# Four 32-row fp32 products for the samples' new SSD states, and B turned by a DMA transpose, in a hybrid attention and SSD layer

## The chip, the cores and the metric

The kernel runs on one core of a Trainium2 chip. The time is the device time of one execution in microseconds (us), taken as the median of several executions. One more execution was recorded by the hardware profiler; durations of single instructions come from that one. TensorE is the matrix engine (PE in the profile; PEld is its weight loads), VectorE is DVE, ScalarE is ACT, GpSimd is POOL, and SP issues most of the DMAs. Each engine works through its own instruction list in order, and semaphores hold an instruction back until what it needs is there. TensorE writes its results to PSUM, from where DVE or ACT must fetch them before the bank can be used again.

## What is computed

One streaming step of one layer serves a prompt of 1024 tokens and 8 samples of 16 tokens each: 1152 tokens together. An input projection feeds a chunk-band attention and a state-space branch (SSD, 32 heads in 4 groups), which are gated, merged and projected. The part that the change touches is the step of the SSD scan, in which each sample is one chunk of 16 tokens:

```python
cb = jnp.einsum('blgn,bsgn->blsg', ck, bk)
...
y_st = jnp.einsum('blgn,bgepn->blgep', ck, h) * jnp.exp(a_cs)[..., None]
to_end = jnp.exp(a_cs[:, -1:] - a_cs)
h_new = h * jnp.exp(a_cs[:, -1])[..., None, None] + jnp.einsum('blgn,blgep->bgepn', bk, xdt * to_end[..., None])
```

`bk` is the matrix B of a group (tokens by 128 states n), `x` the inputs of the heads, `h` the state. For each sample and each pair of heads the second term of `h_new` is a product of B (16 tokens by 128) with the weighted inputs (16 tokens by 128, two heads of 64), summed over 16 tokens. All outputs are fp32.

## The kernel before

**Dense products.** Nearly all of TensorE's time goes into projections whose operands are split into a high and a low fp16 part. One block of 128 output rows takes 3 token groups of 384 columns, 8 slices of the contraction and three matmuls each (L872 high by high, L873 high by low, L875 low by high; L925 to L927 are the same for attention, and L781 to L783 for the last projections, with 288 columns). The results go to three PSUM banks named `d`; three more, `g`, and a double bank, `s`, serve everything else.

**SSD.** After the 8 attention units come 4 groups of 4 pairs of heads. For each group a generator, `group_lat`, prepares what the group's pairs share: B with the tokens on the partitions (`tok`) and the masked product of C and B (`cbm`). B comes out of the convolution with its 128 states on the partitions, so it has to be turned: nine 128 by 128 fp32 transposes on TensorE (L1848), in three rounds that alternate with the products of B and C (L1854); ACT fetches the turned B (L1849) and DVE masks the product (L1856). For each pair, `prelude` makes the decay matrices, and `main` turns the pair's inputs x by a DMA transpose: ACT parts the fp32 words into two planes of 16 bits (L1940), SP starts the transpose (L1942), DVE joins the planes again (L1944). Then come the state products of the prompt (L1990), the outputs within the chunks (L2018, on halves of the array's columns), those from the samples' states (L2025) and from the prompt's (L2038), the store of y (L2055), and at last the samples' new states.

**The samples' new states before.** Two samples of 16 tokens share 32 rows of the 128. B and the weighted inputs `xw` are split into fp32r parts, each 64-row half once as high and once as low: `hi`, `lo` of B once per group (L1962 to L1965), `t` of the inputs per pair (L1971, L1972). GpSimd copies `t` four times with all rows but one sample's masked to zero, two samples in a tile (L1979, `masked(q)`, q = 0 to 3). TensorE then multiplies 128 rows by 256 columns eight times: for each q once with `hi` and once with `lo` (L2063). Only two masked tiles have room, so `masked(2)` and `masked(3)` wait for the products of q = 0 and 1, and there is a pause between the two halves. DVE adds the products to the states (L2072), and they are stored (L2081).

**What sets the order.** Generators record the program with estimated pauses. A list scheduler, class `Order`, then lays out each engine's list once more: from estimated costs of every instruction, it takes the unit that can start first, with a margin after a wait for another engine or a DMA where other work is at hand. So an edit to the SSD part moves instructions on all engines from that place to the end; the order before it, and the set of dense products, stay. Nothing is rearranged when the kernel runs.

**After SSD** come the remaining gate projections, the attention projection with 288 columns, beside which `mod_gate` makes the last modulation vectors (L1004 on quarters of the array's columns, fetched by ACT in L2283, then L1010), and the final projections. ACT's list there also has the splits of the SSD outputs (L2141), which DVE normalises first (L2231) with factors that arrive by a DMA from `yb`.

Of the kernel before, what the change touches and what calls it, by code (L numbers as in the profile page):

```python
# [7 lines left out]
F32 = mybir.dt.float32  # L8
# [3 lines left out]
U16 = mybir.dt.uint16  # L12
I32 = mybir.dt.int32
AF = mybir.ActivationFunctionType
ALU = mybir.AluOpType

P = 128
D = 1024
KT = D // P
NP = 1024  # L20
NB = 8
NS = 16
# [16 lines left out]
TURN = 9000  # L39
# [7 lines left out]

NQL = NQ + 32

C_ID, C_U, C_UB, C_ONE, C_BLK, C_BM, C_SEL, C_S4, C_BM4 = 0, 128, 256, 384, 512, 640, 648, 680, 712  # L50
NCONST = 716

PARAMS = [("norm_g", KT), ("b_ada", 24), ("conv_w", NCV * 4), ("conv_b", NCV), ("qk_g", 2), ("dskip", NPAIR),
          ("ssd_g", NPAIR), ("dt_bias", 32), ("a_log", 32)]
# [366 lines left out]
def trunk_kernel(ctx: ExitStack, tc: tile.TileContext, h, again):  # L421
    nc = tc.nc
# [3 lines left out]
    pss = ctx.enter_context(tc.tile_pool(name="pss", bufs=1, space=bass.MemoryType.PSUM))  # L426
# [4 lines left out]
    rarena = Arena(sb.tile([P, 1280], F32R, name="rarena"), 1280)  # L431
# [4 lines left out]
    def nm(s):  # L436
        uid[0] += 1
        return f"{s}{uid[0]}"

    def pg(cols=512):  # L440
        return psg.tile([P, 512], F32, tag="g", name=nm("g"))[:, :cols]
# [9 lines left out]
    cst = fix(NCONST)  # L451
# [17 lines left out]
    ident = cst[:, C_ID:C_ID + P]  # L469
# [5 lines left out]
    sel = cst[:, C_SEL:C_SEL + 32]  # L475
    sel4 = cst[:, C_S4:C_S4 + 9]
    bmask4 = cst[:, C_BM4:C_BM4 + 4]

    HN = NT // 2
    NSLOT = 12  # L480
# [28 lines left out]
    n = (HCOLS - E0 - 3 * 1184 - 1024) // 1184  # L509
# [5 lines left out]
    more = arena.set_layout(E0 + 1184 + NP + 2048, [("T", 2, NT), ("S", 4, 640)])  # L515
    for tag in more:
        L_ATT[tag] = L_ATT[tag] + more[tag]
    L_ST = rarena.set_layout(0, [("b", 4, P), ("s", 2, P), ("x", 2, 2 * P)])

    def alloc(lay, tag, cols):  # L520
        if lay is L_H or lay is L_W or lay is L_W3 or lay is L_Q or lay is L_V or lay is L_WQ or lay is L_WD:
            return Buf(arena, arena.alloc(lay, tag, cols // 2), cols, True)
        if lay is L_ST:
            return Buf(rarena, rarena.alloc(lay, tag, cols), cols)
        if (lay is L_SSD or lay is L_HEAD or lay is L_TAIL) and tag == "T" or lay is L_HEAD and tag == "Y":
            try:
                return Buf(arena, arena.alloc(L_MORE, "T", cols), cols)
            except NoSlot:
                pass
        return Buf(arena, arena.alloc(lay, tag, cols), cols)  # L530
# [4 lines left out]
    def walloc(lay, tag, cols):  # L535

        while True:
            try:
                return alloc(lay, tag, cols)
            except NoSlot as x:  # L540
                blocked[0] = str(x)
                yield None
# [25 lines left out]
    dma = nc.sync.dma_start  # L568
# [369 lines left out]
    for k in range(KT):  # L938
        b = alloc(L_START, "T", NT)
# [41 lines left out]
    sq = [alloc(L_START, "T", NT) for _ in range(2)]  # L981
# [3 lines left out]
    for k in range(1, KT):  # L985
# [5 lines left out]
        x = xs_in[k].ap  # L991
# [112 lines left out]
    x = xs_in[0]  # L1104
    rp = [psd.tile([P, G3], F32, tag="d", name=nm("d")) for _ in range(3)]
    for g, tok in enumerate(groups):

        for j in range(3):
            late(nc.tensor.matmul(rp[g][:, j * P:(j + 1) * P], v[1][:, 3 * g + j:3 * g + j + 1].to_broadcast([P, P]), ident,
                                  start=True, stop=True))  # L1110
# [12 lines left out]
    sp = pss.tile([P, 2, 512], F32, tag="s", name=nm("s"))  # L1123
# [15 lines left out]
    for k in range(KT):  # L1139
        if k == 0:  # L1140
# [25 lines left out]
            for i in range(3):  # L1166
# [3 lines left out]
                b = wraw[1 + i] = alloc(L_RAW, "raw", 1024)  # L1170
# [58 lines left out]
    def until(t):  # L1229
        while clock[0] < t:  # L1230
            yield -1.0

    def pause(t):
        yield from until(clock[0] + t)
# [78 lines left out]
    def planes(x, at, n):  # L1313
        return x.ap[:, at:at + n * P].bitcast(U16).rearrange("p (t k) -> p t k", t=2)

    def words(x, at, n):
        return x.ap[:, at:at + n * P].bitcast(U16).rearrange("p (k t) -> p t k", t=2)
# [510 lines left out]
    grp = {}  # L1828

    def group_dense(g, lay):  # L1830
        res = grp[g] = {"b": [], "c": [], "sq": None, "st": None}
        yield from conv_gen(16 + g, lay, res["b"])
        yield from conv_gen(20 + g, lay, res["c"])

    def group_lat(g):
        yield from ready(lambda: g in grp and grp[g]["c"] and att_left[0] == 0)
        res = grp[g]
        bt, ct = res["b"][0][0], res["c"][0][0]
        tok = yield from walloc(L_SSD, "T", NT)
        cbm = yield from walloc(L_SSD, "T", NT)  # L1840
        yield from until(res["c"][0][1])
        for j in range(3):
            n = min(4, 9 - 4 * j)
            c = slice(4 * j * P, (4 * j + n) * P)
            pt = pg()
            for s in range(n):
                t0 = (4 * j + s) * P
                nc.tensor.transpose(pt[:, s * P:(s + 1) * P], bt.ap[:, t0:t0 + P], ident)  # L1848
            nc.scalar.activation(tok.ap[:, c], pt[:, :n * P], AF.Copy)  # L1849
            yield 107 * n  # L1850
            pc = pg()
            for s in range(n):
                t0 = (4 * j + s) * P
                nc.tensor.matmul(pc[:, s * P:(s + 1) * P], bt.ap[:, t0:t0 + P], ct.ap[:, t0:t0 + P], start=True, stop=True)  # L1854
            m = (upper if j < 2 else upperb).unsqueeze(1).to_broadcast([P, n, P])
            nc.vector.tensor_tensor(cbm.ap[:, c].rearrange("p (s l) -> p s l", l=P),  # L1856
                                    pc[:, :n * P].rearrange("p (s l) -> p s l", l=P), m, ALU.mult)
            yield 213 * n
        bt.free()
        res["ct"], res["tok"], res["cbm"] = ct, tok, cbm  # L1860
# [3 lines left out]
    def ssd(p):  # L1864
        st = {}
        g = p // PPG
# [60 lines left out]
        def main():  # L1927
            yield from ready(lambda: ssd_all[p] and "z" in st and "cbm" in grp[g] and "t" in dts and st["x"])
            x, tx = st["x"][0]
            z = st["z"]  # L1930
            res = grp[g]
            tokb, ct = res["tok"], res["ct"]
            xd = yield from walloc(lay, "T", NT)
            xw = yield from walloc(lay, "T", NT)
# [17 lines left out]
            me, eb, h0, tm = st["me"]  # L1952
            ssd_all[p + 1] = True

            if res["st"] is None:
                bs = res["st"] = []
                for j in range(2):
                    rw, ro = slice(64 * j, 64 * j + 64), slice(64 - 64 * j, 128 - 64 * j)
                    b_ = tokb.ap[rw, NP:]
                    hi = yield from walloc(L_ST, "b", P)  # L1960
                    lo = yield from walloc(L_ST, "b", P)
                    nc.scalar.activation(hi.r[rw], b_, AF.Copy)  # L1962
                    nc.scalar.activation(hi.r[ro], b_, AF.Copy)
                    nc.vector.tensor_tensor(lo.r[rw], b_, hi.ap[rw], ALU.subtract)
                    nc.vector.tensor_tensor(lo.r[ro], b_, hi.ap[rw], ALU.subtract)  # L1965
                    bs.append((hi, lo))
            xs = []
            for j in range(2):
                rw, ro = slice(64 * j, 64 * j + 64), slice(64 - 64 * j, 128 - 64 * j)
                t = yield from walloc(L_ST, "s", P)  # L1970
                nc.scalar.activation(t.r[rw], xw.ap[rw, NP:], AF.Copy)  # L1971
                nc.vector.tensor_tensor(t.r[ro], xw.ap[rw, NP:], t.ap[rw], ALU.subtract)  # L1972
                xs.append(t)

            def masked(q):

                t = alloc(L_ST, "x", 2 * P)
                i = 2 * (q % 2)
                nc.gpsimd.tensor_tensor(t.r.rearrange("p (b n) -> p b n", n=P), xs[q // 2].ap.unsqueeze(1).to_broadcast([P, 2, P]),  # L1979
                                        bmask4[:, i:i + 2].unsqueeze(2).to_broadcast([P, 2, P]), ALU.mult)  # L1980
                return t

            xm = [masked(0), masked(1)]

            yield from pause(1500)
            for j in range(2):
                ps = pg()
                for s in range(4):
                    c = 4 * j + s
                    nc.tensor.matmul(ps[:, s * P:(s + 1) * P], tokb.ap[:, c * P:(c + 1) * P], xw.ap[:, c * P:(c + 1) * P],  # L1990
                                     start=True, stop=True)
# [64 lines left out]
            nc.scalar.activation(z.ap, x.ap, AF.Square)  # L2056
            stored(x)
            yield from pause(2000)
            pss_ = [pg(), pg()]
            for q in range(4):  # L2060
                j, i = q // 2, q % 2
                for w, b_ in enumerate(res["st"][j]):
                    nc.tensor.matmul(pss_[j][:, 2 * i * P:2 * (i + 1) * P], b_.r, xm[q].r, start=w == 0, stop=w == 1)  # L2063
                xm[q].free()
                if q < 2:
                    xm.append(masked(q + 2))
                yield 215
                if q == 1:
                    yield from pause(4500)
                if i:  # L2070
                    c = slice(4 * j * P, (4 * j + 4) * P)
                    nc.vector.tensor_tensor(h0.ap[:, c], h0.ap[:, c], pss_[j], ALU.add)  # L2072
            for t in xs + [xw]:
                t.free()
            if res["sq"] is None:
                res["sq"] = z
            else:
# [4 lines left out]
            stored(h0)  # L2082
            if p % PPG == PPG - 1:
                s = res["sq"]
                for t in (tokb, res["cbm"], res["ct"], *res["st"][0], *res["st"][1]):
                    t.free()
                yield from pause(4500)
                r0 = drp.tile([1, NT], F32, name=nm("ya"))
                r1 = res["r"] = drp.tile([1, NT], F32, name=nm("yb"))
                yield from token_sums(ones[:, :32], 1, s, r0)  # L2090
                yield from rsqrt_dram(r0, r1, 1, 512, nb)
                if p == NPAIR - 1:
                    dts["x"].free()
# [2133 lines left out]
```

## Time and profile before

| | |
|---|---|
| median of 3 runs | 1749.53 us (1746.5 to 1753.16) |
| the profiled execution: time | 1750.06 us |
| the profiled execution: span of its instructions | 1748.3 us |
| mean granted TensorE clock | 0.995 |
| DMA queue 1 (SP), share of 16 engines | 52.4% |
| SSD part with the remaining gates, us from the start | about 640 to 1360 |

The span begins with the first instruction and ends with the last. In the profile, a row of the groups gives the line of the kernel, the engine, the operation, the tiles and shapes, the count, and then the busy time in us and the mean duration of one in ns. A matmul's duration includes the time until its last result is out, and matmuls overlap; what one costs in a stream is the distance from its start to the start of the next. An fp32 matmul appears as two records (8 records are 4 products); an fp32r or fp16 matmul and a transpose as one. A timeline row gives the start, the length, the engine, line and shapes, the number of instructions merged, and in brackets idle time of the engine with what ended it.

### The profile page before, as it was taken

The page shows a single profiled execution, that of the slowest core. Times are in us where ns is not written, and L with a number is a line of the kernel's source. Part 1 is how long each engine was busy: PE and PEld are TensorE (multiplying, and loading weights), DVE is VectorE, ACT ScalarE, POOL GpSimd, SP SyncE. Part 2 cuts the span into 40 slices and gives each one's busy share as a digit, 9 for nine tenths or more (in the row PEclk, how much of TensorE's full clock was granted, in tenths as well). Part 3 has the DMA queues.
Part 4 walks back from the last instruction along what each step waited for, and adds up shares of the span by engine and source line. Part 5 has one row for each costly group of instructions (what it writes and reads, how often), then busy time and mean ns, then how long its engine had stood idle before and what let it go on. Part 6 is the DMA issues. An engine that isn't in the chain of part 4 may idle for free.

```text
span 1748.3 us, 35611 instructions
## 1 busy us (share of the span) xinstructions
PE 1718.8 (98%) x14013; PEld 1113.4 (64%) x14013; DVE 1312.6 (75%) x2477; ACT 995.8 (57%) x1987; POOL 351.4 (20%) x624
## 2 busy tenths in 40 slices
PE   7999999999999999999999999999999999999998
PEld 3556556556556566667666766676666677666676
DVE  6458667877776967787878777777778787897694
ACT  8766555566465665655755556555666633455340
POOL 0233233224134011232312122212112200000000
PEclk9999999999999999999999999999999999999999
DMA  9248888988878584643554355434555655421141
GB/s 383 76 126 204 191 218 204 200 221 196 203 226 173 148 214 133 171 131 118 170 160 116 118 133 175 140 117 108 155 165 194 244 192 222 146 89 54 58 157 72
DMA packets 267433, 284.92 MB, mean 163 GB/s; under 512 B 199724, under 2 KB 200376, under 8 KB 267256
## 3 DMA queue, kind: packets, MB, share of 16 engines
q1 hardware_dynamic: 258296, 253.90, 52.4%
q0 software_dynamic: 8960, 28.65, 4.4%
q8 instruction: 112, 1.84, 0.4%
q14 instruction: 65, 0.53, 0.1%
HBM read 192.70 MB, written 43.66 MB: 135 GB/s over the span
## 4 chain that ended last, share of the span: by engine, by line
PE 87%; ACT 4%; DVE 4%; DMA 2%; issue 1%; POOL 1%; SPq 0%; DVEq 0%; ACTq 0%; POOLq 0%
PE d L872 16%; PE d L873 16%; PE d L875 16%; PE d L925 5%; PE d L927 5%; PE d L926 5%; PE g L1531 2%; PE s L2018 2%; PE g L1990 2%; PE g L2038 1%; PE s L783 1%; PE s L781 1%; PE s L782 1%; PE s L1578 1%; PE g L1578 1%
## 5 line engine op out<-in xcount | busy, mean ns | idle before, releaser
L872 PE MATMUL d<-arena 128*128 128x384 f16 x1872 | 611.8, 327 | 1.4 <-ACT arena L1706 1.4
L873 PE MATMUL d<-arena 128*128 128x384 f16 x1872 | 610.7, 326 | 0.0
L875 PE MATMUL d<-arena 128*128 128x384 f16 x1872 | 610.7, 326 | 0.0
L875 PEld LDWEIGHTS <-arena 128*128 128x128 f16 x1896 | 185.7, 98 | 122.9 <-issue 0.5
L872 PEld LDWEIGHTS <-arena 128*128 128x128 f16 x1896 | 185.7, 98 | 121.5 <-issue 8.6
L873 PEld LDWEIGHTS <-arena 128*128 128x128 f16 x1896 | 185.7, 98 | 113.5 <-issue 2.0
L628 ACT ACTIVATE arena<-arena 128x1024 bf16<-128x1024 f32 (+4 forms) x185 | 184.6, 998 | 106.1 <-DMA arena<-in_wall_dram 65.4
L925 PE MATMUL d<-arena 128*128 128x384 f16 (+1 forms) x568 | 186.8, 329 | 0.0
L637 DVE SCALAR_TENSOR_TENSOR arena<-arena 128x1024 f16<-128x1024 f32 (+2 forms) x133 | 160.0, 1209 | 35.1 <-ACT arena L636 33.3
L927 PE MATMUL d<-arena 128*128 128x384 f16 (+1 forms) x568 | 186.1, 328 | 0.0
L926 PE MATMUL d<-arena 128*128 128x384 f16 (+1 forms) x568 | 186.1, 328 | 0.0
L636 ACT ACTIVATE arena<-arena 128x1024 f16<-128x1024 f32 (+2 forms) x133 | 135.5, 1021 | 85.3 <-PE d L873 15.5
L1471 ACT ACTIVATE arena<-arena 128x640 f32<-128x640 f32 (+4 forms) x144 | 100.8, 701 | 62.9 <-DVE arena L1474 62.4
L1729 DVE SCALAR_TENSOR_TENSOR arena<-arena 128x1176 f32<-128x1176 f32 x72 | 107.3, 1490 | 2.3 <-issue 0.9
L1917 ACT ACTIVATE arena<-arena 128x128 f32<-128x128 f32 x288 | 89.9, 390 | 25.9 <-DMA arena<-acs_d 25.7
L925 PEld LDWEIGHTS <-arena 128*128 128x128 f16 x576 | 56.3, 98 | 50.8 <-issue 17.5
L1507 DVE SCALAR_TENSOR_TENSOR arena<-arena 128x640 f16<-128x640 f32 (+4 forms) x128 | 87.0, 713 | 0.0
L1366 ACT ACTIVATE arena<-d 128x256 f32<-128x256 f32 x71 | 26.8, 377 | 96.1 <-PE d L927 96.0
L927 PEld LDWEIGHTS <-arena 128*128 128x128 f16 x576 | 56.4, 98 | 38.4 <-issue 0.2
L1399 POOL TENSOR_SCALAR arena<-arena 128x16 f32<-128x16 f32 (+1 forms) x24 | 9.4, 392 | 353.5 <-DVE arena L1372 353.4
L926 PEld LDWEIGHTS <-arena 128*128 128x128 f16 x576 | 56.4, 98 | 32.8
L1474 DVE CUSTOM_DVE_ANT_0 arena<-s,arena 128x320 f32<-128x320 f32 (+4 forms) x128 | 60.3, 503 | 19.4 <-PE s L1578 9.5
(271 smaller groups left out, 3150.0 us busy)
## 6 DMA issues: line engine op xcount, KB each, us to landing
arena<-in_wall_dram SPq DMA_DIRECT2D x85, 512.0 KB
arena<-acs_d SPq DMA_DIRECT2D x32, 576.0 KB
arena<-in_kc_dram SPq DMA_DIRECT2D x64, 256.0 KB
arena<-in_vc_dram SPq DMA_DIRECT2D x64, 256.0 KB
arena<-in_wada_dram SPq DMA_DIRECT2D x24, 512.0 KB
arena<-in_xT_dram SPq DMA_DIRECT2D x16, 576.0 KB
gate_d<-arena POOLq DMA_DIRECT2D x48, 192.0 KB, 3.6
arena<-eacs_d SPq DMA_DIRECT2D x32, 288.0 KB
```

The lines of the kernel that those rows point to most:

```text
L628: keep(nc.scalar.activation(junk[:, :n], x, AF.Square, scale=scale * n ** -0.5, accum_out=sums[:, c:c + 1]))
L636: keep(nc.scalar.activation(hi, x, AF.Copy, scale=scale))
L637: keep(nc.vector.scalar_tensor_tensor(lo, x, scale, hi, ALU.mult, ALU.subtract))
L872: nc.tensor.matmul(ps, hi.r[:, wc], kh.r[:, tok], start=k == 0, stop=False)
L873: nc.tensor.matmul(ps, hi.r[:, wc], kl.r[:, tok], start=False, stop=False)
L875: nc.tensor.matmul(ps, lo.r[:, wc], kh.r[:, tok], start=False, stop=k == nk - 1)
L925: nc.tensor.matmul(ps, kh.r[:, tok], wh, start=k == 0, stop=False)
L926: nc.tensor.matmul(ps, kh.r[:, tok], wl, start=False, stop=False)
L927: nc.tensor.matmul(ps, kl.r[:, tok], wh, start=False, stop=k == KT - 1)
L1471: nc.scalar.activation(p, p, AF.Exp, bias=sm_[:, 4 + e:5 + e], scale=-1.0, accum_out=sm_[:, 6 + e:7 + e])
L1729: nc.vector.scalar_tensor_tensor(yc, r.ap[:, j:j + n], w4[:, i, j:j + 1], yc, ALU.mult, ALU.add)
L1917: nc.scalar.activation(me[e].ap[:, cs], me[e].ap[:, cs], AF.Relu, scale=-1.0, bias=a4[:, c, hds[e]:hds[e] + 1])
```

## The change

B of a group is turned by a DMA transpose of its two 16-bit planes, as the pairs' inputs already were, instead of nine TensorE transposes. For the samples' new states, the split into fp32r parts goes away, on B and on the inputs. GpSimd makes one masked tile per pair (128 rows by 256 columns, of which every 32-row block holds its two samples side by side) with a new constant mask of two columns. TensorE multiplies four blocks of 32 rows, each with its own 32 rows of B, in plain fp32: the four products are addressed to the four row blocks of the array (`tile_position=(32 * j, 0)`) and write to four banks, two `g` and the two halves of `s`. DVE adds them with three instructions instead of two.

```diff
-C_ID, C_U, C_UB, C_ONE, C_BLK, C_BM, C_SEL, C_S4, C_BM4 = 0, 128, 256, 384, 512, 640, 648, 680, 712
-NCONST = 716
+C_ID, C_U, C_UB, C_ONE, C_BLK, C_BM, C_SEL, C_S4, C_BM4, C_BM2 = 0, 128, 256, 384, 512, 640, 648, 680, 712, 716
+NCONST = 718
...
-    L_ST = rarena.set_layout(0, [("b", 4, P), ("s", 2, P), ("x", 2, 2 * P)])
+    L_ST = rarena.set_layout(0, [("x", 2, 2 * P)])
...
         yield from until(res["c"][0][1])
+        nc.scalar.activation(planes(tok, 0, 9), words(bt, 0, 9), AF.Copy)
+        yield from pause(2500)
+        dma(cbm.ap.bitcast(U16).rearrange("p (i k) -> p i k", k=P), tok.ap.bitcast(U16), transpose=True)
+        yield from pause(TURN + 1000)
+        nc.vector.tensor_copy(words(tok, 0, 9), planes(cbm, 0, 9))
+        yield from pause(1800)
         for j in range(3):
             n = min(4, 9 - 4 * j)
             c = slice(4 * j * P, (4 * j + n) * P)
-            pt = pg()
-            for s in range(n):
-                t0 = (4 * j + s) * P
-                nc.tensor.transpose(pt[:, s * P:(s + 1) * P], bt.ap[:, t0:t0 + P], ident)
-            nc.scalar.activation(tok.ap[:, c], pt[:, :n * P], AF.Copy)
-            yield 107 * n
...
-            if res["st"] is None:
-                bs = res["st"] = []
-                for j in range(2):
...
-                    nc.scalar.activation(hi.r[rw], b_, AF.Copy)
-                    nc.scalar.activation(hi.r[ro], b_, AF.Copy)
-                    nc.vector.tensor_tensor(lo.r[rw], b_, hi.ap[rw], ALU.subtract)
-                    nc.vector.tensor_tensor(lo.r[ro], b_, hi.ap[rw], ALU.subtract)
...
-                nc.scalar.activation(t.r[rw], xw.ap[rw, NP:], AF.Copy)
-                nc.vector.tensor_tensor(t.r[ro], xw.ap[rw, NP:], t.ap[rw], ALU.subtract)
...
-            xm = [masked(0), masked(1)]
+            xm = yield from walloc(L_ST, "x", 2 * P)
+            nc.gpsimd.tensor_tensor(xm.ap.rearrange("p (i n) -> p i n", n=P), xw.ap[:, NP:].unsqueeze(1).to_broadcast([P, 2, P]),
+                                    bmask2.unsqueeze(2).to_broadcast([P, 2, P]), ALU.mult)
...
-            pss_ = [pg(), pg()]
-            for q in range(4):
-                j, i = q // 2, q % 2
-                for w, b_ in enumerate(res["st"][j]):
-                    nc.tensor.matmul(pss_[j][:, 2 * i * P:2 * (i + 1) * P], b_.r, xm[q].r, start=w == 0, stop=w == 1)
...
-                if q == 1:
-                    yield from pause(4500)
...
+            sp = pss.tile([P, 2, 512], F32, tag="s", name=nm("s"))
+            pss_ = [pg(2 * P), pg(2 * P), sp[:, 0, :2 * P], sp[:, 1, :2 * P]]
+            for j in range(4):
+                rw = slice(32 * j, 32 * j + 32)
+                nc.tensor.matmul(pss_[j], tokb.ap[rw, NP:], xm.ap[rw], start=True, stop=True, tile_position=(32 * j, 0))
```

The changed file has one line more ahead of `group_lat` and 25 fewer behind `main`, so L872 is now L873, L2063 becomes L2038, L1979 becomes L1957, L1004 becomes L1005 and L2283 becomes L2258.

TensorE's list at the new states of the first pair, before (the first of its two halves; `g_8847` is a bank, `arena` the SBUF):

```order
L875 MATMUL d_8830<-arena 128x384
L2063 MATMUL g_8847<-rarena 128x256 x4
L872 LDWEIGHTS arena
L872 MATMUL d_8830<-arena 128x384
L873 LDWEIGHTS arena
```

and now:

```order
L876 MATMUL d_8916<-arena 128x384
L2038 MATMUL g_8927<-rarena,arena 128x256
L2038 MATMUL g_8928<-rarena,arena 128x256
L2038 MATMUL s_8926<-rarena,arena 128x256 x2
L873 LDWEIGHTS arena
L873 MATMUL d_8916<-arena 128x384
```

Four products stand in one place with dense products on both sides, where eight stood in two places.

GpSimd's list from the store of the second pair's y on, before (L2055 stores y, L1717 to L1719 fetch and store the rows that the convolution leaves, L1979 are the masked tiles, L2081 stores the new states):

```order
L2055 DMA y_d<-arena 128x1152
L1979 TENSOR_TENSOR rarena<-rarena,arena 128x256
L1717 COPY arena<-arena 128x3
L1718 COPY arena<-arena 128x24
L1979 TENSOR_TENSOR rarena<-rarena,arena 128x256
L1719 DMA out_conv_dram<-arena 128x27
L1979 TENSOR_TENSOR rarena<-rarena,arena 128x256 x2
L2081 DMA out_hs_dram<-arena 128x1024
```

and now, from the store of the first pair's y to that of the second's (L2030 stores y, L2056 the new states, L1823 a gate, L1979 is now the store of the prompt's state):

```order
L2030 DMA y_d<-arena 128x1152
L1823 DMA gate_d<-arena 128x384
L2056 DMA out_hs_dram<-arena 128x1024
L1823 DMA gate_d<-arena 128x384
L1718 COPY arena<-arena 128x3
L1719 COPY arena<-arena 128x24
L1720 DMA out_conv_dram<-arena 128x27
L1979 DMA out_hp_dram<-arena 128x128
L2030 DMA y_d<-arena 128x1152
```

No masked tile (L1957) stands between the store of y and the store of the states any more; the two pairs' tiles stand ahead of these rows.

ACT's list ahead of the fetch of `mod_gate`'s first product, before (L816 and L820 fetch products of the attention projection, L636 and L628 work on weights, L2141 splits an SSD output, L2283 is the fetch):

```order
L816 ACTIVATE arena<-s_15353 128x288 x2
L636 ACTIVATE arena<-arena 128x1024
L820 ACTIVATE arena<-d_15356 128x288
L820 ACTIVATE arena<-d_15357 128x288
L2141 ACTIVATE arena<-arena 128x1152
L628 ACTIVATE arena<-arena 128x1152
L628 ACTIVATE arena<-arena 128x1024
L2283 ACTIVATE arena<-g_15517 128x512
```

and now:

```order
L817 ACTIVATE arena<-s_15124 128x288 x2
L637 ACTIVATE arena<-arena 128x1024
L821 ACTIVATE arena<-d_15127 128x288
L821 ACTIVATE arena<-d_15128 128x288
L637 ACTIVATE arena<-arena 128x1024 x2
L2258 ACTIVATE arena<-g_15319 128x512
```

The split of the SSD output now comes after the fetch; two splits of weights stand in its place.

More of the change, by code (lines that the diff above doesn't have):

```diff
@@ L477, in trunk_kernel @@
     bmask4 = cst[:, C_BM4:C_BM4 + 4]
+    bmask2 = cst[:, C_BM2:C_BM2 + 2]
     HN = NT // 2
@@ L1830, in group_dense @@
     def group_dense(g, lay):
-        res = grp[g] = {"b": [], "c": [], "sq": None, "st": None}
+        res = grp[g] = {"b": [], "c": [], "sq": None}
         yield from conv_gen(16 + g, lay, res["b"])
@@ L1953, in main @@
             ssd_all[p + 1] = True
-            if res["st"] is None:
-                bs = res["st"] = []
-                for j in range(2):
[L1958 to L1961, printed above, removed]
-                    nc.scalar.activation(hi.r[rw], b_, AF.Copy)
-                    nc.scalar.activation(hi.r[ro], b_, AF.Copy)
-                    nc.vector.tensor_tensor(lo.r[rw], b_, hi.ap[rw], ALU.subtract)
-                    nc.vector.tensor_tensor(lo.r[ro], b_, hi.ap[rw], ALU.subtract)
[L1966 to L1970, printed above, removed]
-                nc.scalar.activation(t.r[rw], xw.ap[rw, NP:], AF.Copy)
-                nc.vector.tensor_tensor(t.r[ro], xw.ap[rw, NP:], t.ap[rw], ALU.subtract)
[L1973 to L1981, printed above, removed]
-            xm = [masked(0), masked(1)]
+            xm = yield from walloc(L_ST, "x", 2 * P)
+            nc.gpsimd.tensor_tensor(xm.ap.rearrange("p (i n) -> p i n", n=P), xw.ap[:, NP:].unsqueeze(1).to_broadcast([P, 2, P]),
+                                    bmask2.unsqueeze(2).to_broadcast([P, 2, P]), ALU.mult)
             yield from pause(1500)
@@ L2058, in main @@
             yield from pause(2000)
-            pss_ = [pg(), pg()]
-            for q in range(4):
-                j, i = q // 2, q % 2
-                for w, b_ in enumerate(res["st"][j]):
[L2063 to L2067, printed above, removed]
-                if q == 1:
-                    yield from pause(4500)
[L2070 to L2074, printed above, removed]
+            sp = pss.tile([P, 2, 512], F32, tag="s", name=nm("s"))
[3 more added lines that the diff above has]
+                nc.tensor.matmul(pss_[j], tokb.ap[rw, NP:], xm.ap[rw], start=True, stop=True, tile_position=(32 * j, 0))
+            xm.free()
+            xw.free()
+            yield 500
+            for j in range(0, 4, 2):
+                c = slice(4 * j // 2 * P, (4 * j // 2 + 4) * P)
+                c4 = h0.ap[:, c].rearrange("p (b n) -> p b n", b=2)
+                if j:
+                    nc.vector.tensor_tensor(c4, c4, sp[:, :, :2 * P], ALU.add)
+                else:
+                    for i in range(2):
+                        nc.vector.tensor_tensor(c4[:, i], c4[:, i], pss_[i], ALU.add)
             if res["sq"] is None:
@@ L2084, in main @@
                 s = res["sq"]
-                for t in (tokb, res["cbm"], res["ct"], *res["st"][0], *res["st"][1]):
+                for t in (tokb, res["cbm"], res["ct"]):
                     t.free()
@@ L4196 @@
     const[:, C_BM4:C_BM4 + 4] = (i[:, None] // NS) % 4 == np.arange(4)[None, :]
+    const[:, C_BM2:C_BM2 + 2] = (i[:, None] // NS) % 2 == np.arange(2)[None, :]
     ar["const"] = const
```

## The prediction

> **What bounds the kernel now.** I read the page's busy times first, then the chain that ended last, then busy times by stage.
>
> ```profile
> span 1748.3 us, 35611 instructions
> PE 1718.8 (98%) x14013; PEld 1113.4 (64%) x14013; DVE 1312.6 (75%) x2477; ACT 995.8 (57%) x1987; POOL 351.4 (20%) x624
> ...
> PE 87%; ACT 4%; DVE 4%; DMA 2%; issue 1%; POOL 1%; SPq 0%; DVEq 0%; ACTq 0%; POOLq 0%
> ```
>
> ```profile
> 640.00:1360.00 720.00, 717.40 (x5486) 484.37 (x5485) 542.24 (x808) 434.15 (x826) 165.02 (x286) 1.00 0.49 146
> 1360.00:1430.00 70.00, 67.13 (x491) 46.83 (x490) 52.88 (x85) 35.26 (x56) 10.17 (x16) 0.95 0.67 227
> ```
>
> The columns of the second are the stretch, its length, the busy time of PE, PEld, DVE, ACT and POOL, the granted clock, the DMA share and GB/s. In the SSD stretch TensorE is busy 717.4 of 720 us. DVE, with 542, has 178 us of room, ACT and POOL more. So what counts is time on TensorE's own list: instructions taken off it, instructions added, and the few places where it stands still. The end of the program moves by their sum, since dense products follow each of these places.
>
> **What is removed: eight fp32r products per pair.** Groups by form, for counts, then timelines of the first and the last group of four:
>
> ```profile
> L2063 PE MATMUL g<-rarena 128*128 128x256 f32 x128 | 25.9, 320 | 2.6 <-POOL rarena L1979 2.5
> ```
>
> ```profile
> 702.83 0.33 PE L873 MATMUL d<-arena 128*128 128x384 f16 x1
> 702.99 0.33 PE L875 MATMUL d<-arena 128*128 128x384 f16 x1
> 703.02 0.77 PE L2063 MATMUL g<-rarena 128*128 128x256 f32 x4
> 703.63 0.34 PE L872 MATMUL d<-arena 128*128 128x384 f16 x1
> ...
> 1358.52 0.33 PE L875 MATMUL d<-arena 128*128 128x384 f16 x1
> 1358.55 0.77 PE L2063 MATMUL g<-rarena 128*128 128x256 f32 x4
> 1359.16 0.34 PE L872 MATMUL d<-arena 128*128 128x384 f16 x1
> ```
>
> A matmul costs its distance to the next start, for 384 fp16 columns 702.99 - 702.83 = 0.16 us. So four fp32r products cost 703.63 - 702.99 - 0.16 = 0.48 us in the stream, the same at the end. 128 products are 32 groups: **-15.4 us**.
>
> **Removed: 36 transposes.**
>
> ```profile
> 655.20 0.60 PE L1848 MATMUL g<-arena 128*128 128x128 f32 x4
> 655.63 1.06 PE L1854 MATMUL g<-arena 128*128 128x128 f32 x8
> 656.53 0.60 PE L1848 MATMUL g<-arena 128*128 128x128 f32 x4
> ```
>
> Four cost 0.43 us; nine for each of four groups cost 9 x 0.43 = **-3.9 us**.
>
> **Added: four fp32 products on 32 rows per pair.** The same rows price a plain fp32 product: four of L1854 (8 records) in 0.90 us, 0.225 for 128 columns, so 0.45 for 256. No product on 32 rows is in this trace; two nearest kinds are, fp32 on quarters of the columns (L1666) and fp16 on halves of the rows (L1578):
>
> ```profile
> 140.13 0.33 PE L927 MATMUL d<-arena 128*128 128x384 f16 x1
> 140.39 1.30 PE L1666 MATMUL g<-arena 128*32 128x128 f32 x40
> 141.62 0.34 PE L925 MATMUL d<-arena 128*128 128x384 f16 x1
> ...
> 144.56 0.27 PE L1678 MATMUL g<-arena 128*128 128x128 f32 x1
> 144.76 0.58 PE L1578 MATMUL s<-arena 64*128 64x320 f16 x6
> 145.27 0.34 PE L872 MATMUL d<-arena 128*128 128x384 f16 x1
> ```
>
> L1666 is 20 products, five rounds of four. From the end of the dense matmul's turn (140.13 + 0.16) to the next one there are 1.33 us. If a round costs one full product, five are 1.12, and 0.21 remain for entering and leaving the divided array. One after another, 20 would be 4.5 us: columns do run side by side. L1578 is three pairs; after the transpose's 0.11 they take 0.60. At 320/384 of 0.16, three turns are 0.40 if the two halves run together, and 0.20 remain; alone, six would be 0.80. So rows run side by side too, with the same toll of 0.2. What is larger here is the load of weights, exposed once on entry:
>
> ```profile
> L1990 PEld LDWEIGHTS g<-arena x256: 190/192/192, 682.9 to 1334.8; 128*128 128x128 f32 x128
> ...
> L1666 PEld LDWEIGHTS g<-arena x640: 106/110/110, 140.4 to 651.4; 128*32 128x32 f32 x160
> ```
>
> 128 fp32 columns take 0.08 us longer than 32. One round: 0.45 + 0.21 + 0.08 = 0.74 us. Bounds: with nothing extra exposed 0.65; with the second half's weights exposed as well 0.82; all four in turn, 4 x 0.45 + 0.29 = 2.09. I take 0.74, since both near rows show the sharing: 16 x 0.74 = **+11.8 us** (10.4 to 33.4).
>
> [...] The column quarters here agree with a factor near 4 (1.12 of 4.5 us); rows in quarters no run shows yet.
>
> **Removed: a standstill.**
>
> ```profile
> 743.08 0.33 PE L875 MATMUL d<-arena 128*128 128x384 f16 x1
> 743.51 0.50 PE L2063 MATMUL g<-rarena 128*128 128x256 f32 x2
> 746.51 0.80 PE L2063 MATMUL g<-rarena 128*128 128x256 f32 x2 [2.50 <-POOL rarena L1979]
> 747.11 0.54 PE L872 MATMUL d<-arena 128*128 128x384 f16 x1
> ...
> 749.36 0.39 PE L873 MATMUL d<-arena 128*128 128x384 f16 x1
> ```
>
> ```profile
> 744.67 1.22 POOL L1718 COPY arena<-arena 128x24 f32<-128x24 f32 x1
> 745.85 0.61 POOL L1979 TENSOR_TENSOR rarena<-rarena,arena 128x256 fp32r<-128x256 f32 x1
> ```
>
> In the second pair a masked tile came late from GpSimd, behind copies for the convolution. The group took 747.11 - (743.08 + 0.16) = 3.87 us instead of 0.48, and the next seven dense matmuls took 749.36 - 747.11 = 2.25 us instead of 1.14, at half speed: 1.1 more. Together **-4.5 us**. The masked tile of the new kernel is made once, ahead of the store of y, with nothing of TensorE's behind it, so this wait goes.
>
> **Work that lies beside.** Per group, ACT parts B in one pass and DVE joins it in one; the pairs' inputs show the price and the wait for the transpose:
>
> ```profile
> L1940 ACT ACTIVATE arena<-arena x16: 2107/2123/2125, 652.0 to 1299.7; 128x2304 uint16<-128x2304 uint16 x16
> L1942 SPq DMA_TRANSPOSE arena<-arena x16: 2459/2703/4255, 654.1 to 1301.8; - x16
> L1944 DVE COPY arena<-arena x16: 1456/1474/1773, 665.5 to 1308.8; 128x2304 uint16<-128x2304 uint16 x16
> ```
>
> ```profile
> DVE arena L1944 <- DMA arena<-arena: 16.2, 3, 8.0
> ```
>
> That adds 4 x 2.1 us to ACT and 4 x 1.5 to DVE; the small splits (two on ACT and two on DVE for each pair's inputs, and B's) and three of four masks go. DVE's third addition per pair is small beside that. SP is held by each of the four new transposes for 2.7 us, 4.3 at most, with loads of weights queued behind; three blocks are loaded ahead, and each lasts 72 x 0.16 = 11.7 us, so that is covered. DVE's room of 178 us hides its part. `cbm` now comes later in each group, by ACT, transpose and copy; dense products of the next blocks fill TensorE meanwhile, as its list shows. Behind DVE's copy wait the evictions of dense products: three banks `d` of 24 matmuls, 3 x 3.9 us, are the cover. The longest wait, 8.0 us, fitted under it. If the cover fails, it costs as the standstill above, some 4.5 us each.
>
> **The sum** against the profiled execution, 1750.06 us (its span of 1748.3 and 1.8 around it, which I leave as they are; 0.5 above the runs' median): -15.4 - 3.9 + 11.8 - 4.5 = -12.0, so **1738 us**.
>
> **The rivals.** (1) *A second standstill goes too.* In the tail, the chain was DMA, DVE, ACT, TensorE:
>
> ```profile
> 1392.62 1.42 DVE L2231 SCALAR_TENSOR_TENSOR arena<-arena 128x1152 f32<-128x1152 f32 x1 [3.35 <-DMA arena<-yb]
> ```
>
> ```profile
> 1394.08 1.16 ACT L2141 ACTIVATE arena<-arena 128x1152 f16<-128x1152 f32 x1 [6.10 <-DVE arena L2231]
> ```
>
> ```profile
> 1398.24 1.88 PE L1010 MATMUL g<-arena 128*128 128x9 f32 x8 [2.52 <-ACT arena L2283]
> 1399.97 0.40 PE L781 MATMUL g<-arena 128*128 128x288 f16 x1
> ...
> 1404.90 0.29 PE L781 MATMUL d<-arena 128*128 128x288 f16 x1
> ```
>
> The wait is 2.5 us, and the 21 matmuls from 1399.97 to 1404.90 took 4.9 instead of 21 x 0.12 = 2.5 (288 columns at 0.16 for 384): 4.9 us together. ACT's list no longer has the late split (L2141) ahead of the fetch. For: that order; against: an order that is new from the SSD part on makes new tight places. I count one such place as staying: without any, 1733. (2) *New standstills.* One or two more like the one priced, where a unit stands a little too early: 1742.5 to 1747. For: the old order had two in 1100 us; against: POOL's and ACT's lists are emptier. (3) *B's turn comes too late*, slower: at each group's start DVE stands in its copy, evictions wait, all three banks fill, TensorE stops. Four groups at 4.5 us: 1738 + 18 = 1756. It decides from a wait above some 11 us. Against: 8.0 was the longest of 16 such. (4) *The rows do not run together*, so the change isn't what it says: 16 x 2.09 = 33.4, so 1738 + 21.6 = 1759.6, slower. Against: L1578's halves.
>
> **How the numbers follow.** Forecast 0.40, rival 1 0.24, rival 2 0.23, rival 3 0.05, rival 4 0.08. The range of the likeliest alone, from 0.65 to 0.82 a pair, is 1736.5 to 1739.5. For 8 in 10 I reach to rival 1 below and through most of rival 2 above: 1730.5 to 1749. Half a per cent, about what a measurement here can tell from no change, is 8.7 us: below 1740.8 is faster, which takes the forecast's and rival 1's 0.64; within, rival 2 and parts of 3 and 4 between their ends, 0.27; slower 0.09.
>
> **What would show it.** L2038 in a timeline: about 0.74 us between the dense matmuls around it, its records in two bunches of four. 1.3 or more would refute the sharing. No TENSOR_TENSOR of GpSimd as releaser of TensorE. DVE's waits at the four copies of B under 11 us, with no PE idle behind them. L1010 without a wait would be rival 1. PE's busy time down by some 8 us; if it is down and the time is not, new standstills took it, and then the granted clock falls below 1.00 in their stretch.

## The result and the profile after

The changed kernel takes 1735.46 us (median of 5 runs, 1734.17 to 1738.9) where the kernel before took 1749.53 (5 runs, 1746.0 to 1753.16) beside it: ratio 0.9926, 95% interval 0.9912 to 0.9939, or 14.1 us less. The profiled execution took 1734.6 us, 15.5 less than that of before. The forecast was 1738, the range 1730.5 to 1749. The old kernel's time moves with its granted clock: beside the experiments below its executions took from 1742.99 us (clock 0.999) to 1752.61 (0.996), and the profiled one, at 0.995, holds more half speed than most.

The page's head, then busy time by stage (the same two stretches and columns as in the prediction):

```profile
span 1732.7 us, 35395 instructions
PE 1706.9 (99%) x13977; PEld 1094.3 (63%) x13977; DVE 1294.7 (75%) x2449; ACT 982.9 (57%) x1931; POOL 314.4 (18%) x576
```

```profile
640.00:1360.00 720.00, 718.12 (x5511) 471.96 (x5510) 534.49 (x791) 428.91 (x784) 128.65 (x242) 1.00 0.53 155
1360.00:1430.00 70.00, 69.20 (x556) 51.87 (x555) 55.02 (x89) 36.13 (x57) 9.50 (x13) 1.00 0.55 189
```

TensorE is still the bound, with 11.9 us less busy time (1718.8 before). In the tail it is busy 69.2 of 70 us at the full clock, where it had 67.1 at 0.95.

The new products, first pair, in the timeline of TensorE (start, length, shapes, records merged):

```profile
716.22 0.33 PE L876 MATMUL d<-arena 128*128 128x384 f16 x1
716.48 0.48 PE L2038 MATMUL g<-rarena,arena 32*128 32x256 f32 x2
716.49 0.48 PE L2038 MATMUL s<-rarena,arena 32*128 32x256 f32 x2
716.80 0.38 PE L2038 MATMUL g<-rarena,arena 32*128 32x256 f32 x2
716.81 0.38 PE L2038 MATMUL s<-rarena,arena 32*128 32x256 f32 x2
717.13 0.34 PE L873 MATMUL d<-arena 128*128 128x384 f16 x1
```

From the end of the dense matmul's turn (716.22 + 0.16) to the next one there are 0.75 us: four products, eight records in two bunches of four. All 16 pairs measured so make 12.0 us.

TensorE's waits from the SSD part on, and the one at 605 us that before has too (L1707); engine, what it waited for: us in total, times, longest:

```profile
PE d L873 <- ACT arena L1707: 1.4, 1, 1.4
PE d L873 <- DVE arena L1889: 1.3, 1, 1.3
...
PE s L782 <- ACT arena L817: 0.8, 1, 0.8
...
PE g L1855 <- ACT arena L1294: 0.5, 1, 0.5
```

GpSimd's masked tile (L1957) releases nothing in this view. The tail's wait of 2.5 us on the fetch (L2258 now) is gone, and three short standstills are new, at 924 us (1.3), 1003 (0.5) and 1425 (0.8). The one at 924 is an eviction that came late on DVE, timelines of TensorE and DVE:

```profile
922.28 1.95 PE L1965 MATMUL g<-arena 128*128 128x128 f32 x16
925.57 0.32 PE L873 MATMUL d<-arena 128*128 128x384 f16 x1 [1.34 <-DVE arena L1889]
```

```profile
922.23 1.35 DVE L2053 TENSOR_TENSOR arena<-arena 128x1152 f32<-128x1152 f32 x1
...
923.70 1.35 DVE L1924 TENSOR_TENSOR arena<-arena 128x1152 f32<-128x1152 f32 x1
924.97 1.01 DVE L1889 SCALAR_TENSOR_TENSOR arena<-arena,d 128x384 f32<-128x384 f32 x2
```

Two passes over 1152 columns stand right ahead of L1889, which empties the bank that L873 is to open.

**One measure for all runs.** To part work from standing still I took, from the trace, the start of every matmul on the whole array, and subtracted from the distance to the next start what the same shape needs undisturbed (0.1625 us for 384 columns, 0.1225 for 288). What exceeds 0.03 us is *lost time*: standstills, half speed and the loads at the start. The span less the lost time is what the instructions themselves cost, with the waits of products on a part of the array, which this measure leaves in. It depends on what is taken as undisturbed, and its differences are good to about 1 us.

| kernel | span | lost time | span less lost |
|---|---|---|---|
| before | 1748.3 | 40.0 | 1708.3 |
| after | 1732.7 | 32.3 | 1700.4 |
| difference | -15.6 | -7.7 | -7.9 |

So about half of the gain is work and half is time that TensorE no longer lost. By stretches the lost time went from 4.4 to 0.3 us in 700 to 750 (the mask's standstill) and from 8.2 to 2.7 in 1350 to 1450 (the tail's); it rose from 0.2 to 1.8 in 900 to 950 and from 0.2 to 1.0 in 1000 to 1050. The experiments ask whether the work is what the sum says, and whether the standstills went because of the edits or because the order is another one.

### The profile page after: what moved, and what is told of

Its sections match the earlier page's. It is cut to its first block, busy times and chain, and to the rows that moved or that the text cites. A ratio compares the mean times of both kernels' runs of the same rounds, so it can differ in the third digit from the quotient of the medians.

```text
span 1732.7 us, 35395 instructions
## 1 busy us (share of the span) xinstructions
PE 1706.9 (99%) x13977; PEld 1094.3 (63%) x13977; DVE 1294.7 (75%) x2449; ACT 982.9 (57%) x1931; POOL 314.4 (18%) x576
## 5 line engine op out<-in xcount | busy, mean ns | idle before, releaser
L873 PE MATMUL d<-arena 128*128 128x384 f16 x1872 | 610.9, 326 | 2.8 <-ACT arena L1707 1.4
L873 PEld LDWEIGHTS <-arena 128*128 128x128 f16 x1896 | 185.5, 98 | 127.6 <-issue 13.6
```

Of the source, the lines that this page charges most:

```text
L873: nc.tensor.matmul(ps, hi.r[:, wc], kh.r[:, tok], start=k == 0, stop=False)
```

## The experiments

**Each half of the change alone.** Products only: the changed kernel with the old transposes of B.

```diff
-        nc.scalar.activation(planes(tok, 0, 9), words(bt, 0, 9), AF.Copy)
-        yield from pause(2500)
-        dma(cbm.ap.bitcast(U16).rearrange("p (i k) -> p i k", k=P), tok.ap.bitcast(U16), transpose=True)
-        yield from pause(TURN + 1000)
-        nc.vector.tensor_copy(words(tok, 0, 9), planes(cbm, 0, 9))
-        yield from pause(1800)
...
+                nc.tensor.transpose(pt[:, s * P:(s + 1) * P], bt.ap[:, t0:t0 + P], ident)
+            nc.scalar.activation(tok.ap[:, c], pt[:, :n * P], AF.Copy)
```

> The four 32-row products alone; B is still turned by TensorE's transposes. Sum theory: 32 groups of fp32r at 0.48 go (-15.4 us), 16 rounds at 0.75 come (+12.0), the standstill on GpSimd's mask goes (-4.5): 7.9 us below before, 1741.6; 1736.7 if the tail's standstill also goes with the new order. In the trace 36 transposes stay at 0.43 us for four and each pair's products cost 0.75. Rival, that the order's luck alone made the gain: no stable share for the products, time within 3 us of before.

Turn only: the kernel before with the DMA transpose (the same lines the other way round).

> The DMA transpose of B alone; the states are still made by eight fp32r products. Sum theory: 36 transposes go, -3.9 us, 1745.6 where both old standstills (mask 4.5, tail 4.9) stay; down to 1736 if the new order loses both. Rival, that the later B makes TensorE wait at the groups' starts: at or above 1749.5, with idle time of TensorE ended by DVE or a DMA near the four copies.

Measured: 1737.98 us (ratio 0.9939, 0.9915 to 0.9962) and 1739.82 (0.995, 0.9927 to 0.9972), where the kernel before had 1748.55. Neither trace has either of the two large standstills. TensorE's waits with the turn alone, which keeps the fp32r products, the two masked tiles and GpSimd's copies:

```profile
PE g L993 <- DMA arena<-in_xT_dram: 8.4, 3, 7.9
PE s L781 <- ACT arena L816: 2.1, 2, 1.3
PE d L872 <- ACT arena L1706: 1.4, 1, 1.4
PE g L1004 <- DMA arena<-in_wada_dram: 1.3, 1, 1.3
```

All others are 1.2 us or less in total, and no L2063 behind GpSimd is among them: the mask's standstill went with the mask still made the old way. The two gains, 10.6 and 8.7 us, add to more than the whole change's 14.1, since each alone already collects both standstills. Less lost time, the spans are 1704.5 with the turn (3.8 below before; the sum had 3.9) and 1705.9 with the products (2.4 below; the sum had 15.4 - 11.8 = 3.6). In the latter one pair's products cost 2.10 us instead of 0.75, around a wait for B's fetch that my measure doesn't count; with it, 3.7.

**The four products twice.** The changed kernel issues each product two times, and the planner's cost for them is halved, so that no other instruction moves.

```diff
+            t = t / 2 if rows == 32 else t
...
-            for j in range(4):
+            for j in 2 * list(range(4)):
```

> As the changed kernel, with its four products issued twice in a row (the same result is written twice), and the order of all other instructions unchanged. If 0.75 is one round of 0.45 and a toll of 0.3 for entering, leaving and the first weights, a second round adds 0.45: 16 x 0.45 = +7.2 us, 1742.7. If every round pays all of it: +12, 1747.5. If the rows ran one after another: +28.8, 1764.

**All four on one row block.** The same order, with all four products addressed to rows 0 to 31 of the array.

```diff
-                rw = slice(32 * j, 32 * j + 32)
-                nc.tensor.matmul(pss_[j], tokb.ap[rw, NP:], xm.ap[rw], start=True, stop=True, tile_position=(32 * j, 0))
+                rw = slice(0, 32)
+                nc.tensor.matmul(pss_[j], tokb.ap[rw, NP:], xm.ap[rw], start=True, stop=True, tile_position=(0, 0))
```

> As the changed kernel, with all four products on rows 0 to 31 of the array (all four read the first 32 rows of B and of the masked tile, so three quarters of the samples' new states are not computed), and the same order. If the four row blocks are what runs them side by side: 4 x 0.45 + 0.3 = 2.1 us a pair, 16 x 1.35 = +21.6 us, 1757. If the small number of rows suffices, whatever the block: no change, 1735.5.

Measured: 1740.63 us (0.995, 0.9935 to 0.9965) and 1755.39 (1.0041, 1.0028 to 1.0055). The first pair in both, the products twice first:

```profile
715.98 0.33 PE L877 MATMUL d<-arena 128*128 128x384 f16 x1
716.24 0.48 PE L2039 MATMUL g<-rarena,arena 32*128 32x256 f32 x2
716.25 0.48 PE L2039 MATMUL s<-rarena,arena 32*128 32x256 f32 x2
...
716.99 0.38 PE L2039 MATMUL g<-rarena,arena 32*128 32x256 f32 x2
717.00 0.38 PE L2039 MATMUL s<-rarena,arena 32*128 32x256 f32 x2
717.32 0.34 PE L874 MATMUL d<-arena 128*128 128x384 f16 x1
```

```profile
716.16 0.33 PE L876 MATMUL d<-arena 128*128 128x384 f16 x1
716.42 1.12 PE L2038 MATMUL g<-rarena,arena 32*128 32x256 f32 x4
717.39 1.02 PE L2038 MATMUL s<-rarena,arena 32*128 32x256 f32 x4
718.34 0.34 PE L873 MATMUL d<-arena 128*128 128x384 f16 x1
```

A pair now costs 1.18 us twice and 2.02 in turn (median of 16 each). So a second round of four costs 1.18 - 0.75 = 0.43, and 0.75 - 0.43 = 0.32 remain, by my estimate for entering and leaving the divided array. In turn, if the toll is the same, four products take 2.02 - 0.32 = 1.70, or 0.43 each: 3.95 times a round. The time follows: the span less lost time rises by 6.6 us for 16 more rounds of 0.43 (6.9) and by 20.6 for 16 x (2.02 - 0.75) = 20.3. Rows do run side by side here, with 256 columns: by a factor of 3.95, on that estimate, between the round and the four in turn, and of 2.02 / 0.75 = 2.7 with the toll in both.

**The old kernel in another order: margin after GpSimd.** Nothing of the program is changed; the scheduler takes a TensorE unit that reads a GpSimd result as sure only 4000 ns later than before.

```diff
+                    if v["eng"] == "Pool" and u["eng"] == "PE":
+                        m += 4000.0
```

> The kernel before, where the scheduler leaves 4 us more between GpSimd's results and TensorE's use of them if other work is at hand: the second half of the second pair's products stands 48 rows (3.9 us) later on TensorE. If the standstill on the mask costs 4.5 us of the whole: 1745. If dense products behind it only wait elsewhere: 1749.5.

Measured: 1739.6 us (0.9949, 0.9933 to 0.9965), 5.4 below what I expected. Its timeline at the second pair's group (L2065 is the old L2063), then the two stretches:

```profile
745.34 0.77 PE L2065 MATMUL g<-rarena 128*128 128x256 f32 x4
```

```profile
640.00:1360.00 720.00, 719.97 (x5512) 485.61 (x5510) 544.83 (x813) 435.97 (x831) 163.92 (x288) 1.00 0.49 147
1360.00:1430.00 70.00, 69.02 (x547) 50.80 (x545) 57.01 (x92) 35.21 (x56) 7.17 (x13) 1.00 0.69 238
```

The first standstill went, as meant, and the tail's with it, which the edit doesn't name. The rule bears on attention too, so TensorE's order differs from 79 us on, and not only at the masks. In the tail TensorE is busy 69.0 of 70 us, at the full clock. The old arithmetic in this order is 9.3 us faster than in its own. Less lost time its span is 1708.3, the same as before's.

**The tail's products later.** The kernel before, with `mod_gate`'s L1010 recorded behind a pause of 6000 ns for 2000, so that the fetch would be done by then.

```diff
-            yield from pause(2000)
+            yield from pause(6000)
```

> The kernel before, where the modulation sums of the tail (L1010) are recorded 4 us later, so that they stand some 33 matmuls further back on TensorE; the order ahead of the tail is unchanged. If the tail's standstill costs 4.9 us of the whole: 1744.6. If it only moves: 1749.5.

Measured: 1758.39 us (1.0043, 1.0028 to 1.0057): a miss, and to the other side. The wait on the fetch at 1398 went. Elsewhere new ones came. The longest is 4.3 us at 1427, where the next products of `mod_gate` (L1004) wait for their weights from memory, and the granted clock is 0.90 over 1400 to 1450 us. Behind that wait the products of 288 columns start 0.24 us apart (1429.24 to 1429.96), where 0.12 is undisturbed. The other of the two waits in the first row stands at the kernel's start, as in the kernel before:

```profile
PE g L1004 <- DMA arena<-in_wada_dram: 5.6, 2, 4.3
PE g L2063 <- POOL rarena L1979: 2.5, 1, 2.5
```

The mask's standstill is still there, since TensorE's order is the old one up to 1398 us; lost time is 45.9 us. The profiled execution was the longest of the five (1762.21 us). One pause therefore doesn't test the tail's wait by itself; the whole list behind it moved.

**Old and new in three further orders.** The margin of all TensorE units after another engine, 1500 ns for 1000 (old, then new):

```diff
-    SAFE = {"PE": 1000.0, "DVE": 300.0, "Activation": 300.0, "Pool": 0.0, "SP": 300.0}
+    SAFE = {"PE": 1500.0, "DVE": 300.0, "Activation": 300.0, "Pool": 0.0, "SP": 300.0}
```

> The kernel before with the scheduler's margin for TensorE raised from 1000 to 1500: all the same work in another order. It shows how much an order alone moves the time. Sum theory: the time follows the standstills that the trace shows, so 1740 with none of the two to 1754 with another; the price of a group of fp32r products stays 0.48.

> The changed kernel with the same margin of 1500. Sum theory: 7.3 us of TensorE's work below the other order of the old kernel, plus or minus the standstills of either: between 1732 and 1742. If the change's gain were the order's luck, the two would come out alike, within 2 us.

The margin after GpSimd from above, on the changed kernel:

> The changed kernel with the same rule in its scheduler as in the run that gave the old kernel a margin of 4000 ns after GpSimd's results (that one: 1739.6 us, with neither of the two large standstills). Theory A: the change in TensorE's instructions is worth -15.4 - 3.9 + 12.0 = -7.3 us under any order, and the rest of its gain was the old order's standstills. Then this is 1739.6 - 7.3 = 1732.3 us, give or take 2 for small standstills that fall in other places. Rival B: instructions and order can't be parted so; with a clean order the old kernel is as good, and this is 1737 to 1741. Four products of each pair at 0.75 us either way.

And the margin of a bank that has just come free, 2000 ns for 500 (old, then new):

```diff
-    SAFE_SLOT = 500.0
+    SAFE_SLOT = 2000.0
```

> The old kernel with a wider margin for banks (a unit that opens a bank which has only just come free counts as sure 2000 ns after that, not 500). The mask's wait at the samples' new states has nothing to do with a bank, so theory A expects the first standstill to stay (2 to 4.5 us lost there), the tail's to be smaller, and a time of 1742 to 1748 us. If all waits go, 1739.5 as in the two other clean orders of the old products (1739.6, 1739.8).

> The changed kernel with the same wider margin for banks. Its three small standstills (1.5 us at 924, 0.7 at 1003, 1.0 at 1424) are all waits for a bank; if the margin takes them, 1735.5 - 3.2 = 1732.3 us. Theory A: 7.3 us below the old kernel under the same margin, plus what standstills differ. Rival: another order brings as many new ones, 1735 to 1738.

| order | old, us | new, us | difference | span less lost, old | new |
|---|---|---|---|---|---|
| as it was | 1749.53 | 1735.46 | -14.1 | 1708.3 | 1700.4 |
| margin after GpSimd | 1739.6 | 1733.55 | -6.1 | 1708.3 | 1699.8 |
| TensorE margin 1500 | 1745.52 | 1736.71 | -8.8 | 1707.8 | 1699.7 |
| bank margin 2000 | 1747.07 | 1746.29 | -0.8 | 1713.3 | 1705.0 |

Ratios to the kernel before: margin after GpSimd 0.9949 (0.9933 to 0.9965) and 0.9917 (0.9903 to 0.9931); TensorE margin 0.998 (0.9968 to 0.9992) and 0.9927 (0.991 to 0.9943); bank margin 0.9995 (0.9986 to 1.0005) and 0.9994 (0.9981 to 1.0008). The two kernels of the second row were measured beside different executions of the kernel before (medians 1748.9 and 1748.33).

The last column but one and the last differ by 7.9, 8.5, 8.1 and 8.3 us: the work is worth about 8 us in each of these four orders. With the margin after GpSimd the changed kernel's 1733.55 lies within the 2 us that theory A allowed around 1732.3, and below rival B's 1737. The medians differ by anything from 0.8 to 14.1. Under the bank margin both kernels lose 5.1 us to new waits in the attention part, on partial arrays that my measure doesn't hold (its 1713.3 and 1705.0 less these are 1708.2 and 1699.9); the old one's rows:

```profile
PE g L1578 <- DVE arena L1586: 2.3, 1, 2.3
PE g L1666 <- DVE arena L1657: 2.0, 1, 2.0
...
PE g L2063 <- POOL rarena L1979: 1.5, 1, 1.5
...
PE s L1578 <- DVE arena L1474: 0.8, 1, 0.8
```

The new one waits as long at these places, and in place of the mask's wait it has:

```profile
PE d L873 <- DVE arena L1889: 2.8, 1, 2.8
PE g L1579 <- DVE arena L1587: 2.3, 1, 2.3
PE s L782 <- DVE arena L796: 2.0, 2, 1.3
```

It loses 38.3 us, the old one 31.0. I had expected the wider margin to take the three bank waits away: 1732.3, or 1738 at worst. It doubled the largest (L1889) and added others; both readings of that run fell. The changed kernel with the margin after GpSimd, at 1733.55, is the fastest that was run. Whether it is faster than the changed kernel itself stays open, since the intervals of the ratios overlap.

## Why the prediction was right, point by point

- **The fp32r products, -15.4.** A group of four cost a median 0.486 us in the kernels that keep them, 32 times: 15.6.
- **The transposes, -3.9.** 3.8 by the turn alone.
- **Four products, +11.8.** 12.0 measured (0.75 a pair against 0.74). The total was closer than its parts: a round is 0.43 (taken as 0.45), and toll and exposed weights together 0.32 (taken as 0.29). The two near rows, columns in quarters and rows in halves, did price rows in quarters.
- **Work in all.** The three terms give -7.5; -7.9 was measured here, and -8.1 to -8.5 in other orders. What makes up the remaining half microsecond to one was not looked for.
- **The mask's standstill, -4.5.** It went; the lost time of its 50 us fell by 4.1. But the cause that the prediction gave was only one way to lose it: the turn alone and a scheduler margin alone lose it too, with four masked tiles still on GpSimd. With the old products it stood in the other three runs: at 2.5 us with the later tail, whose order is the same up to there, and at 1.7 and 1.5 us under the TensorE margin and the bank margin. That suggests that the place is tight with the old products, and that the order decides what it costs. In none of the seven runs of the new products did it come back.
- **The tail.** This is the step that failed: "I count one such place as staying". None of that size stayed. The tail's lost time fell by 5.5 us although a new wait lost 1.0 at 1424 us: rival 1, and more than its 4.9 us. That price had left out the eight products of L1010 themselves, which took 1.88 us behind the wait and take 0.95 in the changed kernel. The old products lose this wait in every other order that left the tail's program alone (turn alone, and the three margins): the wait hung on one order and was not a property of the tail. That the late split on ACT (L2141) was what decided there was only argued; the one attempt to test the tail alone brought other waits.
- **New standstills (rival 2).** Three came, 3.2 us together (1.5, 0.7 and 1.0 of lost time), each at most a third of the 4.5 us that was priced. So the outcome lies between the forecast and rival 1, and nearer to rival 1: 1734.6 in the profiled execution, between 1738 and 1733.
- **B's turn too late (rival 3).** DVE's copy never waited. Row of the groups, and the longest wait at the pairs' own:

```profile
L1847 DVE COPY arena<-arena 128x2304 uint16<-128x2304 uint16 x4 | 5.9, 1470 | 0.0
```

```profile
DVE arena L1945 <- DMA arena<-arena: 25.3, 7, 9.3
```

  The prices were those of the pairs' inputs (DVE 1.47 us, ACT 2.1, the transpose 2.7 to 3.7). The scheduler starts ACT's part of B's turn 10 to 33 us ahead of the copy (651.6 and 661.9 in the first group, 958.2 and 991.3 in the third), so the cover that the forecast listed wasn't needed there. At the pairs' inputs the longest wait was 9.3 us, above the 8.0 that the forecast went by, and TensorE doesn't stand still behind it.
- **The rows in turn (rival 4).** It would have cost 16 x (2.02 - 0.75) = 20.3 us, and 21.6 was priced; the row blocks are what avoids it.
- **The signs.** 0.75 us and two bunches of four, no GpSimd ahead of TensorE's products, no DVE wait at B: all as listed. PE's busy time fell by 11.9 and not by 8: some 4.5 us of before's came from matmuls at half speed behind the two standstills (1.3 and, with L1010, 3.2 us too long), which count as busy, and 7.9 + 4.5 is 12.4.

## What to carry to other kernels

Price a change to TensorE's work and the standstills of one order apart: here the first was worth about 8 us in four orders, while the order alone moved the old kernel between 1739.6 and 1758.4 us and the new one between 1733.6 and 1746.3. A standstill that hangs on one tight place in a scheduled list may well go, and others come, when anything upstream moves; before a rewrite is credited with it, run the old arithmetic in another order. Four products with 32 rows each belong on four row blocks in one place of the list: here a pair cost 0.75 us so and 2.02 on one row block, and a second round in the same visit cost 0.43 more, not another 0.75.

## What the runs showed of the hardware

**In these traces the length of a wait alone doesn't tell whether half speed follows.** Waits of 2.50 and 2.52 us were followed by matmuls at half speed in the kernel before. The granted clock there was 0.50 from 746.07 to 749.48 us and from 1398.01 to 1404.84. The first of the two and the stretch ahead of it, in which the wait of 2.50 us began, with the columns of the prediction's windows:

```profile
742.65:746.07 3.42, 1.26 (x7) 0.53 (x5) 2.83 (x3) 3.17 (x5) 3.35 (x5) 1.00 0.42 172
746.07:749.48 3.41, 2.97 (x10) 1.70 (x11) 3.41 (x3) 2.97 (x11) 3.16 (x5) 0.50 0.88 269
```

A wait of 2.84 us, in the changed kernel with the bank margin, was not followed by half speed; the starts behind it are 0.16 us apart:

```profile
933.38 0.32 PE L873 MATMUL d<-arena 128*128 128x384 f16 x1 [2.84 <-DVE arena L1889]
933.54 0.32 PE L874 MATMUL d<-arena 128*128 128x384 f16 x1
```

And in the kernel with the later tail products two shorter waits, of 1.45 and 0.35 us, were, but not at once:

```profile
1390.66 0.28 PE L781 MATMUL s<-arena 128*128 128x288 f16 x1 [1.45 <-ACT arena L816]
...
1391.90 0.36 PE L781 MATMUL d<-arena 128*128 128x288 f16 x1 [0.35 <-ACT arena L820]
1392.05 0.45 PE L782 MATMUL d<-arena 128*128 128x288 f16 x1
1392.29 0.45 PE L783 MATMUL d<-arena 128*128 128x288 f16 x1
...
1395.17 0.40 PE L783 MATMUL s<-arena 128*128 128x288 f16 x1
1395.41 0.29 PE L781 MATMUL s<-arena 128*128 128x288 f16 x1
```

Starts are 0.24 us apart from 1392.05 on, and 1395.41 is followed by starts 0.12 apart again; half speed began 1.2 to 1.4 us after the first wait's end (1390.66) and lasted 3.4 us. What decides which waits half speed follows, these runs don't show.
